# An encoder layer with routed experts on one core: the routing of a batch of tiles in two parts, the second part issued three tiles later

## The chip, the cores and the metric

The kernel runs on one core of a Trainium2 chip. The metric is the device time of one execution in microseconds (us); lower is better. The engines are TensorE (PE, with the weight loads PEld beside it), VectorE (DVE), ScalarE (ACT), GpSimd (POOL) and SyncE (SP, which only issues transfers here). Each runs its own instructions in a fixed order and waits on semaphores for the others. POOL also issues the indirect transfers (gathers and scatters by index).

## The reference, cut to what matters

One layer of an encoder on 2048 tokens of width 1024, float32. What the change touches is the part from the output projection to the choice of experts:

```python
y = jnp.concatenate([mix, mem_out], axis=-1) @ w_out        # 768 -> 1024
x = _layer_norm(DEEPNORM_ALPHA * x + y, ln1_g, ln1_b)
gl = t @ wg + bg                  # 4 groups; the best one is taken
el = (t @ we + be)                # 4 experts per group; the best two of the group
top_v, top_i = lax.top_k(el, 2)
ew = softmax(top_v) * gw          # weight of each of the two
# gate[token, expert] = ew at the two experts, else 0
h = silu(t @ w_gate[e]) * (t @ w_up[e]);  moe += gate[:, e] * (h @ w_down[e])
x = _layer_norm(DEEPNORM_ALPHA * x + moe, ln2_g, ln2_b)
```

There are 16 experts of width 256. `mix` comes from a state-space mixer (S5) and `mem_out` from cross-attention to 256 memory tokens; both lie ahead of the change.

## The kernel before

The tokens are 16 tiles of 128. Matrix products are made of float16 halves: `mm3` (L106) issues three matmuls, high by high (L108), high by low (L109), low by high (L110). The program is recorded by a tile framework that orders the instructions of each engine once, when the program is built, by its own estimate of when each could run; on the chip that order is fixed.

`outproj` (L909) runs a loop of 16 + 2 rounds (L972). Round t issues `project(t)` and, two rounds behind (`LAG` = 2), `score(t - 2)`.

- `project(t)` (L932): 36 matmuls into `poo` (two buffers), then `norm` (L871). For tiles 0 to 12 that is: DVE adds the residual and sums (L881), ACT squares (L886), DVE makes the variance (L887), POOL raises it to -1/2 (`rsa`, L898), DVE makes the bias (L904), ACT scales (L905), DVE multiplies by g (L906), POOL adds b (L907, 128 x 1024). For tiles 13 to 15 DVE does the scaling (L900, L901) and POOL only L898. SP stores the tile to `x1d` in memory.
- `score(t)` (L949): PE transposes the tile (`turn_rows` L982, `ptr`), ACT and DVE copy it to `xT` (for tiles below 12 in two float16 halves, the low one by DVE at L996), PE multiplies by the router's weights (`pl`), DVE adds the bias (`lg`, L961). `pl` has one buffer.

Tiles are routed in batches: (0,4), (4,4), (8,2), (10,2), (12,2), (14,2), as first tile and count. After a batch's last tile `score` calls `route` (L1052). Its first half, some 35 small DVE rows, finds the group and the two experts and ends with the matrix A of ones at the chosen experts (L1112). Then PE multiplies A by a triangle and by ones (L1116 to L1119, into `pp`, one buffer), which gives each pair's place in its expert's list; DVE adds the running counts (`run_cnt`) and works out the places (L1121 to L1144); and POOL scatters the token numbers to the lists in memory, `listd`, two indirect transfers for each tile (L1149): eight for a batch of four, four for a batch of two.

After tile 9 (`EARLY_T` = 10) `early_rows` (L999) loads the lists of two experts (`idx`, SP) and gathers their first 128 tokens each (`xk`, POOL, L1201). `early` (L1006) then transposes them (`ptre`) and runs those experts' first tile ahead of the others; in the fixed order of PE this comes among the scores of the last tiles. `moe` (L1250) loads all lists (`idxall`, `idxrem`) when the last batch has been scattered, gathers the experts' tokens (`xg`, `xr`) and computes the experts (from `ptr` at L1458 on). `pz` (L1260) are two buffers that POOL sets to zero for it.

Of the kernel before, what the change touches and what calls it, by code (L numbers as in the profile page):

```python
# [21 lines left out]
NT = 16  # L22
# [21 lines left out]
EARLY_T = 10  # L44
# [28 lines left out]
class Kern:  # L73
# [32 lines left out]
    def mm3(self, ps, lh, ll, rh, rl, first, last):  # L106
        mm = self.nc.tensor.matmul
        mm(ps, lh, rh, start=first, stop=False)  # L108
        mm(ps, lh, rl, start=False, stop=False)  # L109
        mm(ps, ll, rh, start=False, stop=last)  # L110

    def run(self):
        with ExitStack() as top:
# [795 lines left out]
    def outproj(self):  # L909
        nc, a = self.nc, self.a  # L910
        V = nc.vector
        self.scat, self.oscat, self.sts, self.lds = [], [], [], []
        self.nw = 0
        with ExitStack() as o:
            wp = o.enter_context(self.pool("wout", side="left"))
            kp = self.kp = o.enter_context(self.pool("outk", bufs=2, side="left"))
            ps = o.enter_context(self.pool("psout", bufs=2, space=PSUM))
            self.rps = o.enter_context(self.pool("psr", bufs=1, space=PSUM))
            wh = wp.tile([P, 6, D], F16, name="owh")
            wl = wp.tile([P, 6, D], F16, name="owl")  # L920
            for c in range(6):
                raw = kp.tile([P, D], F32, tag="xres", name=f"oraw{c}")
                nc.sync.dma_start(raw, a["w_out"][:, c])
                (self.split_w_q if c in OWQ else self.split_w)(wh[:, c], wl[:, c], raw)
            g1 = wp.tile([P, D], F32, name="g1")
            b1 = wp.tile([P, D], F32, name="b1")
            nc.sync.dma_start(g1, a["ln1_g"])
            nc.sync.dma_start(b1, a["ln1_b"])
            x1 = {}
            logits = {}  # L930

            def project(t):  # L932
                tk = slice(t * P, t * P + P)
                xr = kp.tile([P, D], F32, tag="xres", name=f"xres{t}")
                nc.sync.dma_start(xr, a["x"][t])
                r = x1[t] = kp.tile([P, D], F32, tag="r1", bufs=4, name=f"r1_{t}")
                po = ps.tile([P, D], F32, tag="po", name=f"poo{t}")
                for c in range(6):
                    if c < 4:
                        lh, ll = self.mh[:, c, tk], self.ml[:, c, tk]  # L940
                    else:
                        lh, ll = self.OTh[:, c - 4, tk], self.OTl[:, c - 4, tk]
                    for n in range(2):
                        ns = slice(n * 512, n * 512 + 512)
                        self.mm3(po[:, ns], lh, ll, wh[:, c, ns], wl[:, c, ns], c == 0, c == 5)
                self.norm(kp, r, xr, WS * ALPHA, po, EPS * WS * WS, g1, b1, f"a{t}", HOW1[t])
                nc.sync.dma_start(self.x1d[tk], r)

            def score(t):  # L949
                whole = t >= WHOLE_T  # L950
                xT = self.turn_rows(x1[t], f"{t}", whole)
                pl = self.rps.tile([P, 20], F32, tag="pl", bufs=1, name=f"pl{t}")
                for c in range(DC):
                    if whole:
                        nc.tensor.matmul(pl, xT[:, c], self.wrf[:, c], start=(c == 0), stop=(c == DC - 1))
                    else:
                        self.mm3(pl, xT[0][:, c], xT[1][:, c], self.wr[0][:, c], self.wr[1][:, c], c == 0, c == DC - 1)
                t0, n = self.batch[t]
                if t == t0:
                    logits[t0] = kp.tile([P, 4, 20], F32, tag="lg", name=f"lg{t}")  # L960
                V.scalar_tensor_tensor(logits[t0][:, t - t0], pl, 1.0 if whole else 1.0 / WS, self.rb, op0=ALU.mult, op1=ALU.add)  # L961
                if t == t0 + n - 1:
                    self.route(kp, logits[t0][:, 0:n], t0, n)
                if t == EARLY_T - 1:
                    self.early_rows(kp)

            self.batch = {}
            for t0, n in BATCHES:
                for t in range(t0, t0 + n):
                    self.batch[t] = (t0, n)  # L970
            LAG = 2
            self.W = [self.expert_weights(self.load_weights(e), e, self.split_w_pool) for e in range(EARLY)]  # L972
            for t in range(NT + LAG):
                if t < NT:
                    project(t)
                if t >= LAG:
                    score(t - LAG)
            for e in range(EARLY):
                self.early(e, ps)

# [71 lines left out]
    def route(self, kp, lg, t0, n):  # L1052
# [4 lines left out]
        def T(shape, dt=F32, bufs=2):  # L1057
            k[0] += 1
            return kp.tile([P] + shape, dt, tag=f"rt{k[0]}", bufs=bufs, name=f"rt{t0}_{k[0]}")

        def first_max(v, shape, m2=None):

            mx = T(shape[:-1])
            V.tensor_reduce(mx, v, axis=AX.X, op=ALU.max)
            eq = T(shape)
            V.tensor_tensor(eq, v, mx.unsqueeze(2).to_broadcast([P] + shape), op=ALU.is_equal)
            V.tensor_tensor(eq, eq, self.w4.unsqueeze(1).to_broadcast([P] + shape), op=ALU.mult)
            m2 = T(shape[:-1]) if m2 is None else m2
            V.tensor_reduce(m2, eq, axis=AX.X, op=ALU.max)
            V.tensor_tensor(eq, eq, m2.unsqueeze(2).to_broadcast([P] + shape), op=ALU.is_equal)  # L1070
            return mx, eq, m2
# [14 lines left out]
        m1, o1, _ = first_max(e1, [n, 4], im[:, :, 0])  # L1086
        e2 = T([n, 4])
        V.scalar_tensor_tensor(e2, o1, -1e30, e1, op0=ALU.mult, op1=ALU.add)
        m2, o2, _ = first_max(e2, [n, 4], im[:, :, 1])
# [20 lines left out]
                            oh.unsqueeze(2).to_broadcast([P, n, 4, 4]), op=ALU.mult)  # L1110
        A = T([n, NE], F16)
        V.tensor_tensor(A, sel[:, :, 0], sel[:, :, 1], op=ALU.add)  # L1112
        pp = self.rps.tile([P, n + 1, NE], F32, tag="pp", bufs=1, name=f"pp{t0}")
        for i in range(n):
            for q in range(i):
# [476 lines left out]
```

## Time and profile before

| | |
|---|---|
| median of 3 executions | 1093.28 us (1093.13 to 1101.6) |
| the profiled execution's own time | 1091.53 us |
| its span, from the first to the last instruction | 1089.7 us |
| PE busy | 899.5 us (83%) |
| PEld busy | 606.8 us (56%) |
| DVE busy | 828.3 us (76%) |
| ACT busy | 540.5 us (50%) |
| POOL busy | 535.3 us (49%) |
| mean granted clock of PE | 0.931 of full speed |
| HBM read, written | 141.95 MB, 58.49 MB |

Times within the trace count from the span's start. In it the projections run from about 488 to 655 us, the last scores and routings to about 702, and the MoE's gathered experts from there to the end. The granted clock is the share of full speed that the chip allowed PE. A wait is shown with its releaser, the row on another engine whose end set the last semaphore; "issue" means that nothing in the profile shows a wait. In a timeline each row has start, length, engine, line, operation, output and inputs, and in square brackets the idle time of the engine just ahead of it. Matmuls overlap, so their pitch is read from their starts.

### The profile page before, as it was taken

The numbers are of one execution on the slowest core, as the hardware profiler recorded it, in microseconds if no ns is written. First come the engines' busy times: TensorE is split into PE (matmuls) and PEld (weight loads), VectorE is DVE, ScalarE is ACT, GpSimd is POOL, SyncE is SP. The second block draws the span as 40 slices with busy tenths as digits, with TensorE's granted clock in tenths as the row PEclk, the third lists the DMA queues.
The fourth block names the chain that finished last, engine by engine and source line by source line (L and its number), as shares of the span: only waits on it lengthen the run. The fifth ranks groups of instructions, "written<-read, shape, count | busy, mean of one in ns | idle before, by whom it ended". The sixth has DMA issues, their size and how long they took to land. (4 is left out here: it accounts for less than half of the span.)

```text
span 1089.7 us, 18757 instructions
## 1 busy us (share of the span) xinstructions
PE 899.5 (83%) x7108; PEld 606.8 (56%) x7108; DVE 828.3 (76%) x1636; ACT 540.5 (50%) x1068; POOL 535.3 (49%) x379
## 2 busy tenths in 40 slices
PE   7777599985845999899999888698979987989880
PEld 4444465674734877444554447476657754755540
DVE  7999888969997666483585676467878787878774
ACT  5122243445748776477633312265656554746530
POOL 1475655426663331325945444525444566367454
PEclk9899799999887999999999987899999998999995
DMA  7113355275271422417736331476578669557531
GB/s 253 41 45 117 121 180 202 69 243 168 61 227 46 132 81 77 140 55 267 257 141 116 78 114 64 142 292 227 206 269 319 215 225 334 198 205 233 208 107 65
DMA packets 65199, 178.14 MB, mean 163 GB/s; under 512 B 15121, under 2 KB 33425, under 8 KB 57681
## 3 DMA queue, kind: packets, MB, share of 16 engines
q1 hardware_dynamic: 44800, 128.83, 36.2%
q0 software_dynamic: 20304, 48.07, 12.9%
q8 instruction: 57, 0.93, 0.3%
q14 instruction: 38, 0.30, 0.1%
HBM read 141.95 MB, written 58.49 MB: 184 GB/s over the span
## 5 line engine op out<-in xcount | busy, mean ns | idle before, releaser
L92 DVE SCALAR_TENSOR_TENSOR wl<-raw,wh 128x1024 f16<-128x1024 f32 x82 | 97.8, 1219 | 10.4 <-ACT wh L91 7.9
L91 ACT ACTIVATE wh<-raw 128x1024 f16<-128x1024 f32 x82 | 82.0, 1048 | 24.1 <-PE pg L109 13.8
L109 PE MATMUL pg<-xl,wh 128*128 128x288 f16 (+1 forms) x256 | 73.3, 288 | 3.0 <-DVE xl L1462 2.8
L110 PE MATMUL pg<-xh,wl 128*128 128x288 f16 (+1 forms) x256 | 73.3, 288 | 0.9 <-issue 0.9
L108 PE MATMUL pu<-xh,wh 128*128 128x288 f16 (+1 forms) x256 | 71.8, 283 | 2.4 <-DVE hl L1049 1.9
L108 PE MATMUL pg<-xh,wh 128*128 128x288 f16 (+1 forms) x256 | 73.5, 289 | 0.0
L1206 POOL DMA_INDIRECT xs<-xg,idxall x31 | 38.9, 1256 | 70.2 <-DVE xg L1499 40.9
L110 PE MATMUL pu<-xh,wl 128*128 128x288 f16 (+1 forms) x256 | 71.6, 282 | 1.5 <-issue 1.5
L109 PE MATMUL pu<-xl,wh 128*128 128x288 f16 (+1 forms) x256 | 71.6, 282 | 0.0
L109 PEld LDWEIGHTS <-wh 128*128 128x128 f16 x576 | 58.1, 101 | 19.0 <-issue 5.7
L108 PEld LDWEIGHTS <-wh 128*128 128x128 f16 x576 | 58.3, 101 | 18.5 <-issue 3.5
L110 PEld LDWEIGHTS <-wl 128*128 128x128 f16 x576 | 57.9, 101 | 17.5 <-issue 4.4
L108 PE MATMUL pq<-xh,S 128*128 128x128 f16 x256 | 51.0, 235 | 15.9 <-DVE OT L295 15.9
L743 POOL TENSOR_TENSOR pe<-pe,ri 128x1024 f32<-128x1024 f32 x16 | 30.3, 1895 | 55.5 <-DVE ri L742 38.8
L108 PE MATMUL pu<-winh,xh 128*128 128x512 f16 x128 | 49.7, 388 | 6.6 <-ACT winh L91 6.6
L1201 POOL DMA_INDIRECT xg<-x1d,idxall x31 | 37.9, 1222 | 32.9 <-DMA out_x<-xg,idxall 13.0
L108 PE MATMUL py<-wh,hh 128*128 128x512 f16 x120 | 45.9, 385 | 8.8 <-ACT hh L1048 4.6
L1462 DVE TENSOR_TENSOR xl<-pt,xh 128x512 f16<-128x512 f32 x60 | 39.5, 683 | 16.1 <-ACT xh L1461 10.1
L1461 ACT ACTIVATE xh<-pt 128x512 f16<-128x512 f32 x60 | 34.0, 592 | 35.8 <-PE pt L1458 29.5
L110 PE MATMUL pq<-xh,S 128*128 128x128 f16 x256 | 51.2, 235 | 0.4 <-DVE S L92 0.3
L1458 PE MATMUL pt<-ident,xg 128*128 128x128 f32 x240 | 37.8, 285 | 16.5 <-DVE xl L1462 7.6
L691 POOL TENSOR_TENSOR m<-S,R 128x1024 f32<-128x1024 f32 x10 | 30.4, 3045 | 42.0 <-DVE S L715 23.6
(471 smaller groups left out, 3163.6 us busy)
## 6 DMA issues: line engine op xcount, KB each, us to landing
raw<-in_w_gate SPq DMA_DIRECT2D x16, 1024.0 KB
raw<-in_w_up SPq DMA_DIRECT2D x16, 1024.0 KB
raw<-in_w_down SPq DMA_DIRECT2D x16, 1024.0 KB
xr<-in_xT SPq DMA_DIRECT2D x16, 512.0 KB
xs<-wo SPq DMA_DIRECT2D x16, 512.0 KB
wol<-xs SPq DMA_DIRECT2D x16, 512.0 KB
M<-kd SPq DMA_DIRECT2D x64, 128.0 KB
xres<-in_x SPq DMA_DIRECT2D x16, 512.0 KB
```

The source lines that it names most:

```text
L91: self.nc.scalar.activation(hi, raw, AF.Copy, scale=WS)
L92: self.nc.vector.scalar_tensor_tensor(lo, raw, WS, hi, op0=ALU.mult, op1=ALU.subtract)
L108: mm(ps, lh, rh, start=first, stop=False)
L109: mm(ps, lh, rl, start=False, stop=False)
L110: mm(ps, ll, rh, start=False, stop=last)
L691: Q.tensor_tensor(m[:, 1], S[:, :, 1::-1], tab(1), op=ALU.mult)
L743: nc.gpsimd.tensor_tensor(pe, pe, ri.unsqueeze(2).to_broadcast([P, 4, 256]), op=ALU.mult)
L1201: return self.nc.gpsimd.indirect_dma_start(out=out, out_offset=None, in_=src, in_offset=bass.IndirectOffsetOnAxis(ap=idx, axis=0))
L1206: st = self.nc.gpsimd.indirect_dma_start(out=self.xs, out_offset=bass.IndirectOffsetOnAxis(ap=si, axis=0), in_=z[:sz], in_offset=None, bou ...
L1458: nc.tensor.transpose(pt[:, i, off:off + sz], x[:sz, (d0 + i) * P:(d0 + i) * P + P], self.ident[:sz, :sz])
L1461: nc.scalar.activation(xh[:, ds_, :n], pt, AF.Copy)
L1462: nc.vector.tensor_tensor(xl[:, ds_, :n], pt, xh[:, ds_, :n], op=ALU.subtract)
```

## The change

`route` becomes a generator that stops after A. `score` runs it to there and puts the rest on a list with the batch's last tile t. Each round of the loop calls `place(t)` between `project` and `score`: the rest of a batch whose last tile lies `LAG` + 3 = 5 rounds back is issued there, so three tiles after the round in which its first part was issued. It is issued inside `issue_after(self.projected)`, which orders the PE instructions of the block behind the last matmul of the projection just issued; `mm3` returns that matmul for it. The early rows are issued with the rest of batch 8. What is left after the loop follows at once (`place(2 * NT)`). The second parts of batches 0, 4, 8 and 10 so come after projections 8, 12, 14 and 15, those of 12 and 14 after all scores. From `route` on, the line numbers of the kernel of after are 14 or 15 higher (L1117 becomes L1132, L1149 becomes L1164, L1201 becomes L1216, L991 becomes L1005).

```diff
@@ mm3
-        mm(ps, ll, rh, start=False, stop=last)
+        return mm(ps, ll, rh, start=False, stop=last)
@@ outproj, project
-                        self.mm3(po[:, ns], lh, ll, wh[:, c, ns], wl[:, c, ns], c == 0, c == 5)
+                        self.projected = self.mm3(po[:, ns], lh, ll, wh[:, c, ns], wl[:, c, ns], c == 0, c == 5).ins
@@ outproj, score
                 if t == t0 + n - 1:
-                    self.route(kp, logits[t0][:, 0:n], t0, n)
-                if t == EARLY_T - 1:
-                    self.early_rows(kp)
+                    rest = self.route(kp, logits[t0][:, 0:n], t0, n)
+                    next(rest)
+                    places.append((t, rest))
+
+
+            def place(now):
+                while places and places[0][0] + LAG + 3 <= now:
+                    t, rest = places.pop(0)
+                    with self.tc.issue_after(self.projected):
+                        for _ in rest:
+                            pass
+                    if t == EARLY_T - 1:
+                        self.early_rows(kp)
+
+            places = []
@@ outproj, the loop
                 if t < NT:
                     project(t)
+                place(t)
                 if t >= LAG:
                     score(t - LAG)
+            place(2 * NT)
@@ route
         V.tensor_tensor(A, sel[:, :, 0], sel[:, :, 1], op=ALU.add)
+        yield
         pp = self.rps.tile([P, n + 1, NE], F32, tag="pp", bufs=1, name=f"pp{t0}")
```

TensorE, around the prefix sums of batch 4 (`pp_6481`), in the kernel before. They stand among the logits of tile 8 (`pl_6605`), and projection 11 (`poo_6635`) goes on behind them:

```order
L109 MATMUL pl_6605<-wr_5311,xT_6590 128x20
L1117 LDWEIGHTS tri
L1117 MATMUL pp_6481<-rt_19_6479,tri 128x16
L1116 LDWEIGHTS ones
L1116 MATMUL pp_6481<-rt_19_6479,ones 128x16
```

In the kernel of after the same sums (`pp_6779`) stand between the last matmul of projection 12 (`poo_6727`) and the transpose of tile 10 (`r_10`):

```order
L109 MATMUL poo_6727<-owl,OT 128x512
L110 LDWEIGHTS OT
L110 MATMUL poo_6727<-owh,OT 128x512
L1132 LDWEIGHTS tri
L1132 MATMUL pp_6779<-rt_19_6479,tri 128x16
```

The sums have moved behind the rest of projection 11 and all of projection 12, and the logits of tile 8 have nothing between them any more.

POOL, in the kernel before, from the power of tile 10 on (of the `listd` rows, x8 are batch 4's lists, the first x4 batch 8's and the second batch 10's; the `rsa` rows shown are the powers of tiles 10, 11, 13 and 14; `xk` are the gathers of the early rows; `pz` the memsets):

```order
L898 TENSOR_TENSOR rsa_6575<-vaa_6577,mhalf 128x1
L907 TENSOR_TENSOR r_10_6537<-r_10_6537,b_5384 128x1024
L1149 DMA listd<-rt_17_6472,rt_28_6520 32768x4 x8
L898 TENSOR_TENSOR rsa_6672<-vaa_6674,mhalf 128x1
...
L898 TENSOR_TENSOR rsa_6961<-vaa_6963,mhalf 128x1
L1149 DMA listd<-rt_17_6769,rt_28_6809 32768x4 x4
L1201 DMA xk_5340<-x1d,idx_6820 128x1024
L1201 DMA xk_5341<-x1d,idx_6820 128x1024
L898 TENSOR_TENSOR rsa_7145<-vaa_7147,mhalf 128x1
L1260 MEMSET pz_7784 128x1024
L1260 MEMSET pz_7786 128x1024
L1149 DMA listd<-rt_17_7055,rt_28_7094 32768x4 x4
```

and in the kernel of after, from the power of tile 12 on:

```order
L898 TENSOR_TENSOR rsa_6764<-vaa_6766,mhalf 128x1
L1164 DMA listd<-rt_17_6472,rt_28_6818 32768x4 x8
L907 TENSOR_TENSOR r_12_6726<-r_12_6726,b_5384 128x1024
L898 TENSOR_TENSOR rsa_6915<-vaa_6917,mhalf 128x1
L898 TENSOR_TENSOR rsa_7058<-vaa_7060,mhalf 128x1
L1164 DMA listd<-rt_17_6715,rt_28_7101 32768x4 x4
L1275 MEMSET pz_7784 128x1024
L1275 MEMSET pz_7786 128x1024
L898 TENSOR_TENSOR rsa_7180<-vaa_7182,mhalf 128x1
L1216 DMA xk_5340<-x1d,idx_7112 128x1024
L1216 DMA xk_5341<-x1d,idx_7112 128x1024
L1164 DMA listd<-rt_17_7009,rt_28_7295 32768x4 x4
```

Batch 4's lists moved from behind tile 10's add to between the power and the add of tile 12 (batch 0's moved likewise, from ahead of tile 7's add to ahead of tile 8's); batch 8's lists moved behind the powers of tiles 13 and 14; the power of tile 15 (`rsa_7180`), which stood behind batch 10's lists, now stands ahead of the gathers `xk`, and batch 10's lists come last of these.

TensorE at the end of the scores, in the kernel before: the logits of tile 15 (`pl_7384`, two halves of four matmuls), the transposes of the gathered rows (`ptre`) and the sums of batch 12 (`pp_7306`):

```order
L955 MATMUL pl_7384<-wr,xT_7371 128x20 x4
L991 MATMUL ptre_0_7486<-ident,xk_5340 128x128 x4
L1117 LDWEIGHTS tri
L1117 MATMUL pp_7306<-rt_19_7304,tri 128x16
...
L955 MATMUL pl_7384<-wr,xT_7371 128x20 x4
L991 MATMUL ptre_1_7493<-ident,xk_5340 128x128 x4
```

and in the kernel of after (`pl_7343`, and `pp_7403` for batch 12):

```order
L955 MATMUL pl_7343<-wr,xT_7330 128x20 x4
L1005 MATMUL ptre_0_7486<-ident,xk_5340 128x128 x4
L955 MATMUL pl_7343<-wr,xT_7330 128x20 x4
L1005 MATMUL ptre_1_7493<-ident,xk_5340 128x128 x4
L1132 LDWEIGHTS tri
L1132 MATMUL pp_7403<-rt_19_7263,tri 128x16
```

The transposes of the gathered rows stay where they stood; the sums of batch 12 moved behind them.

## Rows read from the trace of the kernel before

**Rows 1.** Windows: length, busy PE, PEld, DVE, ACT, POOL; clock; DMA share; GB/s

```profile
655.00:702.00 47.00, 33.76 (x318) 28.69 (x317) 28.40 (x160) 11.63 (x23) 21.23 (x21) 0.79 0.23 69
702.00:1090.00 388.00, 321.05 (x2475) 224.87 (x2473) 299.13 (x464) 205.20 (x361) 197.23 (x160) 0.93 0.64 224
651.00:676.00 25.00, 20.52 (x128) 17.38 (x128) 16.71 (x108) 6.34 (x13) 9.47 (x10) 0.64 0.30 106
```

**Rows 2.** Waits of PE, 488 to 725: total us, times, longest

```profile
PE pp L1117 <- DVE rt L1112: 11.4, 4, 4.8
PE ptr L1458 <- DMA xr<-x1d,idxrem: 7.1, 1, 7.1
```

**Rows 3.** Timeline of PE: start, us, row, idle before; sums and transposes

```profile
600.58 0.17 PE L1117 MATMUL pp<-rt,tri 128*128 128x16 f16 x1 [2.50 <-DVE rt L1112]
...
625.42 0.17 PE L1117 MATMUL pp<-rt,tri 128*128 128x16 f16 x1 [2.56 <-DVE rt L1112]
...
651.60 0.17 PE L1117 MATMUL pp<-rt,tri 128*128 128x16 f16 x1 [4.82 <-DVE rt L1112]
...
668.76 1.09 PE L991 MATMUL ptre<-ident,xk 128*128 128x128 f32 x4
...
701.52 1.94 PE L1458 MATMUL ptr<-ident,xr 128*128 128x128 f32 x8 [7.05 <-DMA xr<-x1d,idxrem]
```

**Rows 4.** Timeline of PE: matmuls of projections 11, 12 and 15

```profile
602.26 0.63 PE L108 MATMUL poo<-owh,OT 128*128 128x512 f16 x1
602.68 0.63 PE L109 MATMUL poo<-owl,OT 128*128 128x512 f16 x1
...
614.25 0.38 PE L109 MATMUL poo<-owl,OT 128*128 128x512 f16 x1
614.47 0.38 PE L110 MATMUL poo<-owh,OT 128*128 128x512 f16 x1
...
654.67 0.63 PE L110 MATMUL poo<-owh,OT 128*128 128x512 f16 x1
```

**Rows 5.** Timeline of POOL: lists, add of tile 12, gathers, memsets, power of tile 15

```profile
606.60 1.03 POOL L1149 DMA_INDIRECT listd<-rt,rt  x1 [2.24 <-DVE rt L1144]
...
615.53 0.96 POOL L1149 DMA_INDIRECT listd<-rt,rt  x1 [0.30 <-issue]
...
628.28 2.35 POOL L907 TENSOR_TENSOR r<-r,b 128x1024 f32<-128x1024 f32 x1 [3.27 <-issue]
...
641.52 0.96 POOL L1149 DMA_INDIRECT listd<-rt,rt  x1 [0.30 <-issue]
647.28 0.98 POOL L1201 DMA_INDIRECT xk<-x1d,idx  x1 [4.79 <-DMA idx<-listd]
...
655.37 1.84 POOL L1260 MEMSET pz<- 128x1024 f32 x2 [5.24 <-PE poo L110]
...
663.15 0.59 POOL L898 TENSOR_TENSOR rsa<-vaa,mhalf 128x1 f32<-128x1 f32 x1
...
684.09 1.04 POOL L1149 DMA_INDIRECT listd<-rt,rt  x1 [6.10 <-DVE ovs_le L1187]
...
695.64 0.98 POOL L1201 DMA_INDIRECT xr<-x1d,idxrem  x1 [0.48 <-issue]
```

**Rows 6.** Timeline of DVE: a held row, logits, scaling of tile 15, last list row

```profile
602.24 2.34 DVE L1128 TENSOR_TENSOR rt<-rt,rt 128x64 f32<-128x64 f32 x2
...
616.56 0.18 DVE L961 SCALAR_TENSOR_TENSOR lg<-pl,rb 128x20 f32<-128x20 f32 x1 [6.95 <-PE ptr L991]
...
663.77 1.28 DVE L901 SCALAR_TENSOR_TENSOR r<-r,rsa,b 128x1024 f32<-128x1024 f32 x1 [1.63 <-POOL rsa L898]
...
671.74 0.18 DVE L961 SCALAR_TENSOR_TENSOR lg<-pl,rb 128x20 f32<-128x20 f32 x1
...
683.57 0.24 DVE L1144 SCALAR_TENSOR_TENSOR rt<-rt,tok 128x4 int32<-128x4 f32 x2
```

**Rows 7.** DMA queues, 647 to 651 us: packets, MB, share of 16 engines

```profile
q0 software_dynamic: 145, 0.55, 46.3%
```

## The prediction, made before the changed kernel ran

> **What bounds the kernel now.** I read four views in turn: busy time by stage, the waits of TensorE in the stretch that the change touches, then the timelines of TensorE, GpSimd (POOL) and VectorE (DVE) there. The stage table shows where something can be won: in the stretch from the last projection to the first expert, 655 to 702 us, PE is busy 33.8 of 47 us and its granted clock is 0.79, while the MoE behind it (702 to 1090) keeps PE at 321 of 388 us [rows 1]. The change alters nothing that the MoE computes, so its value is the time by which the MoE's first transpose comes earlier.
>
> From the projections' start to the first expert (488 to 725 us) PE waits 11.4 us in four pieces for the first matmul of a batch's prefix sum (pp): about 1.5 us for batch 0, then 2.50, 2.56 and 4.82 us for batches 4, 8 and 10 [rows 2, 3]. The releaser is A, the last DVE row of the routing's first part. The only other long wait is the 7.05 us for the gathered rows xr at the MoE's door [rows 2, 3].
>
> **What goes.** The four waits: 11.4 us. Behind three of them PE runs at half rate for a while: matmuls of 512 columns start 0.42 us apart at 602.26, against 0.22 at 614.25, which are the levels of 1.2 and 2.4 GHz [rows 4]. I count eight at 0.21 us too much behind batch 4 (1.7 us), about 1.3 behind batch 8, and, as the last row of projection 15 at 654.67 is 0.63 us long like those at 602.26 and not 0.38, about 1.7 behind batch 10 (half of the stretch from 651.60 on); together 4.7 us. The stretch 651 to 676 shows the same as a clock of 0.64 [rows 1]. So PE gets back at most 16.1 us. One further wait goes: tile 15's power (rsa, 663.15) stood on POOL behind the two memsets (655.37) and batch 10's four lists; in the new order no lists of batch 10 stand ahead of it. At most it waited for all four, 5.1 us by the price below, which brings the upper bound to about 21 [rows 5].
>
> **What comes, batch 0 and 4.** No instruction is added on any engine (the returned matmul and the generator exist only while the program is built), but the sums, the small DVE rows and the lists' transfers all move. One list takes 0.96 us and 0.30 us until the next: batch 4's eight start at 606.60 and 615.53, so 1.27 us each, 10.1 us for eight, 5.1 for four [rows 5]. Batch 0's eight now stand ahead of tile 8's bias add and tile 9's power, which DVE awaits in the middle of batch 4's first part, with tile 8's casts behind. So of the 5.7 us at stake around the first two waits (1.5 + 2.5 + 1.7) between 0 and 5.7 come back; I take 3, the middle. Projection 12, which ended at 614.47 + 0.38 = 614.85 [rows 4], then ends at 611.8.
>
> From there to projection 15's end (654.67 + 0.63 = 655.3) it took 40.45 us [rows 4]. Batches 8 and 10 give back 2.56 + 4.82 + 1.3 + 1.7 = 10.4. But batch 4's lists now stand between tile 12's power and its add. The pp matmuls come at 611.8; in the trace the first list follows pp by 606.60 - 600.58 = 6.0 us, of which one DVE row of 2.34 was held while POOL added [rows 3, 5, 6]. DVE has tile 12's sum and square ahead of it, so I set the first list at 621.5 (617.8 if nothing is ahead). The eight end at 631.6, the add (2.35) at 634; before it ended at 628.28 + 2.35 = 630.6 [rows 5]. SP's load of the early lists moves behind loads that wait for projection 15's end, which is in time for lists that come later still. PE comes to tile 12's transpose at about 631 and waits 3 us (bounds 0 and 6). Projection 15 ends at 611.8 + 40.45 - 10.4 + 3 = 644.9, 10.4 us earlier.
>
> **Batch 8, the early rows and tile 15.** Lists of batch 8 start when its second part is through DVE, which has tile 13's scaling in its middle and that waits for the power behind batch 4's add (634 + 0.6, then 1.28 for the scaling and 8.1 us of small rows, by two thirds of the 12.1 us that both parts of a batch of two took from its last logits at 671.74 to the end of the row at 683.57): 644.0 [rows 5, 6]. They end at 649.1. Next on POOL come the memsets, 1.84 us, and tile 15's power, 0.59: 651.5; tile 15 is scaled at 652.8, where before it was 663.77 + 1.28 = 665.05. Its last logits (lg) would follow as before by 671.74 - 665.05 = 6.7 us, at 659.5 [rows 6].
>
> But PE's order puts the second half of tile 15's logits behind the transpose of the gathered rows xk, before and now. Their gather starts one round trip after the last list, 647.28 - 642.48 = 4.8 us: 653.9. How long it takes to land is not shown by itself. The queue moved 0.55 MB by 651, one gather and a little more, 3.7 us after its start at 647.28; the gather xr took from 695.64 to PE's start at 701.52, 5.9 us, with others beside it [rows 3, 5, 7]. I take 4.2, nearer the first since nothing else is on the queue: 658.1, and 2.4 us for four transposes (1.09), the other half of the logits and the row that makes lg: 660.5 [rows 3]. So the wait for xk takes 1.0 us of tile 15's gain (0.5 to 2.7).
>
> The Trainium skill (DMA: Bandwidth & Descriptors, "Anatomy of one DMA — SWDGE (gpsimd) path") gives about 2.0 us fixed and the bytes over 436e9 per second. For 512 KB that is an estimate of 3.2 us, which the trace's 3.7 for a little more allows; by it tile 15 itself would set its logits (659.5) and the time would come out 1.0 us shorter, 1083.1.
>
> **The tail.** From lg at 671.74 to the last batch's DVE row (683.57 + 0.24) were 12.1 us; some eleven more DVE rows of batch 12's second part now stand in between, about 1 us. 660.5 + 13.1 + 0.3 = 673.9 for the first list of batch 14, against 684.09 [rows 5, 6]. The two gathers and the lists of batches 10 and 12 (5.1 us each) fill POOL from 653.9 to 666.6 at the earliest, so POOL itself leaves 7 us there. From that list to the MoE's first transpose it stays 701.52 - 684.09 = 17.4 us [rows 3, 5]. Gain 10.2. PE stands still at three new places (tile 8's casts, tile 12's add, xk: about 3, 3 and 2 us), and half rate may follow there as in [rows 4]; I take off 1 us, about two thirds of what one such wait cost before. **Sum: 9.2 us**; the profiled execution had 1091.53 us with a span of 1089.7 (1.8 lie around it), so 1082.3, and on the median of 1093.28, which is 1.75 higher, 1084.0.
>
> **Rivals.** *A, the waits come back whole.* Lists issue while PE has other work and the add of tile 12 is early enough: 16.1 us of PE less about 1.6 for xk's bound, a gain of 14.5, 1079. For it: the first list could start at 617.8, and then the add is in time. Against it: one POOL queue holds all lists and the adds.
> *B, the wait moves to the POOL block.* DVE stands 6.95 us ahead of tile 9's lg at 616.56, longer than I can derive from what stands ahead of it [rows 6]; one such wait in either of the two stretches that I walk (some 4 us each beyond what I counted) leaves a gain of 1: 1092.
> *C, slower: the round trip of xk.* Early rows used to be fetched from batch 8's lists at 647.28, 16 us before tile 15 was scaled; now 1 us behind it. If batch 8's lists end after about 659, xk lands after 668, and the end is later than before by every us more: with the lists' end at 663, 4 us, 1097. For it: two DVE-POOL-DVE handovers stand ahead of these lists. Against it: my walk has 10 us to spare.
>
> **How the numbers follow.** My forecast (gain 4 to 12, from the bounds of batch 0, tile 12's add and xk: 1081 to 1089.5) gets 0.50, A 0.27, B 0.15, C 0.08. Beyond 1097 or below 1075 hardly anything is left; leaving out half of C and the ends of A, 1076 to 1096 holds some 8 in 10. About 1% (10.9 us) is what a measurement can tell from no change. Faster by over 1%, below 1082.3: all of A and about a fifth of the forecast, 0.37; slower by over 1%, above 1104, would need batch 8's lists to end at 670, half of C, 0.04; within 1%: 0.59.
>
> **What would show it.** No wait of PE at pp; a wait at tile 12's transpose for POOL's add; DVE's scaling of tile 13 waiting for its power near 635; tile 15 scaled near 652.8; a wait of PE for xk that ends near 658; the last batch's first list near 673.9 and xr's transpose near 691.3. A first MoE transpose above 700 would say B or C; one below 688 would say A. If the MoE itself (388 us before) changes by more than 2 us, the premise that it only shifts is wrong.

## The result, and the profile after

The changed kernel takes 1078.0 us (median of 6 executions, 1077.3 to 1085.1) beside 1093.2 for the kernel before (1090.0 to 1101.6): a ratio of 0.989 with a 95% interval of 0.986 to 0.992, so it is 9 to 16 us faster. A second series gave 1083.7 (9 executions) beside 1094.3, ratio 0.990 (0.986 to 0.994). The forecast was 1084.0 and 1076 to 1096.

| | before | after |
|---|---|---|
| profiled execution / its span | 1091.53 / 1089.7 us | 1077.70 / 1075.9 us |
| PE, DVE busy | 899.5, 828.3 us | 896.7, 825.0 us |
| POOL busy | 535.3 us | 537.4 us |
| mean granted clock | 0.931 | 0.931 |

The engines do the same work; what went is waiting. To see where, I cut each profile at two instants: the first matmul of the first projection, and the MoE's first transpose. In the kernel of after, from the timeline of PE (start, length, row, idle before):

```profile
484.92 0.38 PE L108 MATMUL poo<-owh,mh 128*128 128x512 f16 x1
...
686.89 1.97 PE L1473 MATMUL ptr<-ident,xr 128*128 128x128 f32 x8 [5.96 <-DMA xr<-x1d,idxrem]
```

and in the kernel before the first of the two (the second is in [rows 3], at 701.52):

```profile
488.12 0.38 PE L108 MATMUL poo<-owh,mh 128*128 128x512 f16 x1
```

So the profiled execution's 13.8 us are three pieces: 3.2 us ahead of the first projection, where the two programs are the same row for row on every engine; 11.4 us between the two instants (213.4 to 202.0); and 0.8 us lost in the MoE (388.2 to 389.0). I call the middle piece **the stretch**; the experiments are read from it. Times below with a plus sign count from the first projection's first matmul.

The waits of PE in the same window as [rows 2] (line waited at, releaser: total us, times, longest):

```profile
PE ptr L1473 <- DMA xr<-x1d,idxrem: 6.0, 1, 6.0
PE pl L110 <- DVE xT L1010: 2.5, 4, 0.8
PE ptre L1005 <- DMA xk<-x1d,idx: 2.2, 1, 2.2
...
PE ptr L1005 <- POOL r L907: 1.9, 2, 1.5
```

The 11.4 us at pp are gone. Two of the announced new waits stand there: for xk, and for POOL's add at tile 12's transpose, half as long as I had it. The sums now start right behind a projection, with no idle time ahead of them:

```profile
605.75 0.17 PE L1132 MATMUL pp<-rt,tri 128*128 128x16 f16 x1
...
627.27 1.09 PE L1005 MATMUL ptr<-ident,r 128*128 128x128 f32 x8 [1.48 <-POOL r L907]
...
651.84 1.09 PE L1005 MATMUL ptre<-ident,xk 128*128 128x128 f32 x4 [2.19 <-DMA xk<-x1d,idx]
...
664.15 0.17 PE L1132 MATMUL pp<-rt,tri 128*128 128x16 f16 x1 [0.34 <-issue]
```

POOL's timeline, to be set beside [rows 5]: the first of batch 4's lists, tile 12's add, the last of batch 8's lists, the memsets, tile 15's power, the first gather of early rows and the first list of batch 14:

```profile
614.00 1.98 POOL L1164 DMA_INDIRECT listd<-rt,rt  x1 [1.80 <-DVE rt L1159]
...
624.86 2.36 POOL L907 TENSOR_TENSOR r<-r,b 128x1024 f32<-128x1024 f32 x1
...
640.26 1.74 POOL L1164 DMA_INDIRECT listd<-rt,rt  x1 [0.30 <-DVE vaa L887]
642.00 1.86 POOL L1275 MEMSET pz<- 128x1024 f32 x2
643.81 0.57 POOL L898 TENSOR_TENSOR rsa<-vaa,mhalf 128x1 f32<-128x1 f32 x1
647.40 1.02 POOL L1216 DMA_INDIRECT xk<-x1d,idx  x1 [3.02 <-issue]
...
669.48 0.97 POOL L1164 DMA_INDIRECT listd<-rt,rt  x1 [5.45 <-DVE ovs_po L1204]
```

And DVE, beside [rows 6]: the scaling of tile 15, its logits, and the last row of the last batch's first part (A), which the sums at 664.15 use:

```profile
644.41 1.29 DVE L901 SCALAR_TENSOR_TENSOR r<-r,rsa,b 128x1024 f32<-128x1024 f32 x1 [2.06 <-POOL rsa L898]
...
654.49 0.18 DVE L961 SCALAR_TENSOR_TENSOR lg<-pl,rb 128x20 f32<-128x20 f32 x1
...
661.16 0.19 DVE L1126 TENSOR_TENSOR rt<-rt 128x32 f16<-128x32 f32 x1
```

The steps of the forecast, on the common zero (the forecast's instants less 488.1, the rows of after less 484.9):

| us after the first projection's first matmul | before | forecast | after |
|---|---|---|---|
| projection 12 ends | 126.7 | 123.7 | 121.0 |
| first list of batch 4 | 118.5 | 133.4 | 129.1 |
| tile 12's add ends | 142.5 | 145.9 | 142.3 |
| projection 15 ends | 167.2 | 156.8 | 152.1 |
| tile 15 scaled | 176.9 | 164.7 | 160.8 |
| gather of xk starts | 159.2 | 165.8 | 162.5 |
| transpose of xk starts | 180.6 | 170.0 | 166.9 |
| last logits | 183.6 | 172.4 | 169.6 |
| first list of batch 14 | 196.0 | 185.8 | 184.6 |
| MoE's first transpose | 213.4 | 203.2 | 202.0 |

### The profile page after: what moved, and what is told of

Its sections match the earlier page's. It is cut to its first block, busy times and chain, and to the rows that moved or that the text cites. A ratio compares the mean times of both kernels' runs of the same rounds, so it can differ in the third digit from the quotient of the medians.

```text
span 1075.9 us, 18762 instructions
## 1 busy us (share of the span) xinstructions
PE 896.7 (83%) x7108; PEld 607.8 (56%) x7108; DVE 825.0 (77%) x1636; ACT 540.8 (50%) x1068; POOL 537.4 (50%) x379
## 5 line engine op out<-in xcount | busy, mean ns | idle before, releaser
L91 ACT ACTIVATE wh<-raw 128x1024 f16<-128x1024 f32 x82 | 82.0, 1048 | 23.3 <-PE pg L109 12.2
L1216 POOL DMA_INDIRECT xg<-x1d,idxall x31 | 39.2, 1266 | 32.6 <-DMA out_x<-xg,idxall 14.5
L109 PE MATMUL pq<-xl,S 128*128 128x128 f16 x256 | 50.1, 233 | 0.0
L109 PE MATMUL pu<-winl,xh 128*128 128x512 f16 x128 | 49.4, 386 | 0.3 <-DVE winl L92 0.3
```

The lines of the kernel that those rows point to most:

```text
L91: self.nc.scalar.activation(hi, raw, AF.Copy, scale=WS)
L1216: return self.nc.gpsimd.indirect_dma_start(out=out, out_offset=None, in_=src, in_offset=bass.IndirectOffsetOnAxis(ap=idx, axis=0))
```

## Experiments

Each was profiled, and timed against the kernel before. All milestones are from the timelines, as in the table above. "Total" is the ratio to the kernel before with its 95% interval; the kernel before was timed again in each series, and its median ran from 1087.7 to 1094.3 us there, so totals compare as ratios only.

| | proj. 12 ends | proj. 15 ends | last logits | last lists start | MoE starts (the stretch) | MoE's length | total |
|---|---|---|---|---|---|---|---|
| before | 126.7 | 167.2 | 183.6 | 196.0 | 213.4 | 388.2 | |
| before again | 126.5 | 167.1 | 183.4 | 195.9 | 213.2 | 394.7 | 1.002 (0.999, 1.005) |
| after | 121.0 | 152.1 | 169.6 | 184.6 | 202.0 | 389.0 | 0.989 (0.986, 0.992) |
| after again | 121.0 | 152.0 | 169.4 | 186.0 | 203.0 | 390.3 | 0.990 (0.986, 0.994) |
| 0 and 4 at once | 126.8 | 156.9 | 174.4 | 189.6 | 206.6 | 394.2 | 0.994 (0.991, 0.997) |
| held five tiles | 118.9 | 152.1 | 174.4 | 191.6 | 209.6 | 391.6 | 0.994 (0.992, 0.997) |
| held one tile (the program of before, see below) | 126.4 | 167.4 | 183.5 | 196.1 | 214.9 | 395.6 | 1.002 (1.000, 1.004) |
| early rows later, no hold | 127.0 | 158.5 | 173.9 | 187.8 | 205.8 | 398.0 | 1.000 (0.997, 1.003) |
| batch 8 held two tiles | 121.5 | 151.9 | 168.4 | 184.4 | 202.2 | 395.5 | 0.995 (0.992, 0.998) |
| tile 12's add on DVE | 122.5 | 151.9 | 172.1 | 184.0 | 201.9 | 396.1 | 0.996 (0.994, 0.999) |
| early experts last | 120.7 | 151.8 | 166.3 | 177.7 | 210.6 | 396.5 | 0.997 (0.994, 1.000) |
| the same, batches 8 and 12 sooner | 121.6 | 151.8 | 167.7 | 177.8 | 210.8 | 397.2 | 1.001 (0.998, 1.005) |
| second early expert last | 121.0 | 152.0 | 169.5 | 182.4 | 200.8 | 393.9 | 0.994 (0.991, 0.998) |
| the same, batch 8 held two tiles | 121.0 | 151.2 | 167.9 | 183.1 | 200.5 | 398.4 | 0.992 (0.989, 0.996) |

**How far a profile can be trusted.** The two kernels once more, unchanged.

> The changed kernel once more, for a second profile. Theory: the stretch from the first projection to the MoE's first transpose is fixed by the order (202.0 within 1 us), while what lies ahead (484.9 us) and the MoE behind (389.0 us) move by several us from one execution to the next. Rival: the stretch itself varies by as much as the others.

> The kernel before once more, for a second profile. Theory: the stretch is again 213.4 within 1 us, ahead of it 485 to 488 us, and the MoE between 388 and 396. Rival: the changed kernel's lower time ahead of the stretch (484.9 against 488.1) comes from the change: then it is 488 again here.

Both stretches came again: 213.2 after 213.4, and 203.0 after 202.0 (up to the last logits within 0.3). The first projection began at 485.7 in the kernel before and at 487.8 in the changed one, the other way round than in the first pair. So the 3.2 us ahead of the stretch were no effect of the change, and the rival falls. The MoE of the same kernel before took 388.2 and 394.7. The largest single difference between these two that I can name is DVE's wait for one scattered and gathered tile, pzr. Waits of DVE, 700 to 850 us, in the two profiles of before:

```profile
DVE pzr L881 <- DMA pzr<-xs,idxrem: 6.6, 1, 6.6
```

```profile
DVE pzr L881 <- DMA pzr<-xs,idxrem: 10.3, 1, 10.3
```

In the two of after it was 12.2 and 6.8, with MoEs of 389.0 and 390.3, so this wait alone does not set the MoE's length. A difference of 5 us in the total says little from one execution; the stretch says it to 1 or 2 us (a third profile of the same program, below, has 214.9).

**Is it the waits for the sums, and which of them?** Batches 0 and 4 are routed at once, the others held.

```diff
                     next(rest)
-                    places.append((t, rest))
+                    if t in (3, 7):
+                        for _ in rest:
+                            pass
+                        if t == EARLY_T - 1:
+                            self.early_rows(kp)
+                    else:
+                        places.append((t, rest))
```

> Batches 0 and 4 are routed at once, as in the kernel before; batches 8 to 14 are held as in the changed kernel. Measure: the time from the first projection's first matmul to the MoE's first transpose (before 213.4 us, changed 202.0). Theory: the gain is the four waits of TensorE for the sums plus the half rate behind them, less what waits anew; the waits of batches 0 and 4 (1.5 + 2.5 us) and 1.7 us at half rate come back: 207.7, time some 5.7 us above the changed kernel. Rival: the gain comes from GpSimd and VectorE, where the powers of tiles 14 and 15 no longer stand behind the early rows' gather and batch 10's lists; then batches 0 and 4 are worth at most 1 us here: 202 to 203.

The stretch is 206.6, 4.1 above the mean of after's two (202.5). Projection 12 ends where it did before (126.8), 5.8 us later than in after, and PE waits 4.0 us in two pieces for the sums again:

```profile
PE pp L1138 <- DVE rt L1132: 4.0, 2, 2.5
```

So 5.8 us at projection 12 are the first two waits (1.5 and 2.5) and the half rate behind the second (1.7: eight matmuls run 0.42 us apart again), all of it; and the rest of the gain, 6.7 us of the stretch, comes with the batches from 8 on.

**Is a shorter hold enough?** `LAG + 1` in place of `LAG + 3`.

```diff
-                while places and places[0][0] + LAG + 3 <= now:
+                while places and places[0][0] + LAG + 1 <= now:
```

> Every second part is held one tile instead of three. In TensorE's order the sums of batches 4 and 8 then stand in the logits of a tile as in the kernel before, those of batch 10 inside projection 15. Same measure. Theory: the wait of batch 4 (2.5 us and 1.7 at half rate) stays, that of batch 8 is gone since a tile more lies ahead of it, that of batch 10 is gone or small, and the gathers stand ahead of tile 14's power again: 205 to 209. Rival (any hold is enough): 202 to 203.

The stretch is 214.9 and nothing is won, but this run tests neither expectation. With this edit the tile framework gives every engine the same instructions in the same order, with the same semaphores, as in the kernel before: its own estimate puts the rows that were issued a tile later back where they stood. Batch 10's sums, too, stand in the middle of projection 15 in the kernel before, with eight of its matmuls directly on either side. So the run is a third profile of the kernel before, and a hold of one tile was never executed. It is of use all the same: in it PE waits 10.3 us for the sums, 3.8 of them for batch 10's, and DVE's timeline says what that wait hangs on, with the scaling of tile 14 ahead of the rest of that batch's first part:

```profile
PE pp L1132 <- DVE rt L1126: 10.3, 4, 3.8
```

```profile
648.75 1.28 DVE L901 SCALAR_TENSOR_TENSOR r<-r,rsa,b 128x1024 f32<-128x1024 f32 x1 [6.15 <-POOL rsa L898]
```

The power that this row waits for stands on POOL behind the two gathers, which wait 5.18 us for the list to come back from memory:

```profile
645.87 0.98 POOL L1216 DMA_INDIRECT xk<-x1d,idx  x1 [5.18 <-DMA idx<-listd]
647.15 0.95 POOL L1216 DMA_INDIRECT xk<-x1d,idx  x1 [0.30 <-issue]
648.13 0.58 POOL L898 TENSOR_TENSOR rsa<-vaa,mhalf 128x1 f32<-128x1 f32 x1
```

The first profile of the kernel before has the same chain, with POOL's wait of 4.79 us at 647.28 [rows 5]. POOL's power of tile 14, DVE's scaling and A of batch 10 there:

```profile
649.54 0.59 POOL L898 TENSOR_TENSOR rsa<-vaa,mhalf 128x1 f32<-128x1 f32 x1
```

```profile
650.16 1.28 DVE L901 SCALAR_TENSOR_TENSOR r<-r,rsa,b 128x1024 f32<-128x1024 f32 x1 [5.77 <-POOL rsa L898]
651.37 0.18 DVE L1112 TENSOR_TENSOR rt<-rt 128x32 f16<-128x32 f32 x1
```

**So is it the early rows?** The kernel before with one condition changed; nothing is held.

```diff
-                if t == EARLY_T - 1:
+                if t == 11:
                     self.early_rows(kp)
```

> The kernel before with one thing changed: the early rows (load of idx and gathers xk) are issued after tile 11 instead of tile 9, so that on GpSimd they stand behind the powers of tiles 14 and 15 and batch 10's lists. No second part is held. Same measure (before 213.4 and 213.2). Theory: the longest wait of TensorE for the sums, 4.8 to 5.1 us for batch 10, is GpSimd's wait for idx (4.8 us) handed on by the power of tile 14 and the scaling that stands in the middle of batch 10's first part; it goes with the 1.7 us at half rate, projection 15 ends 5 to 6.5 us earlier (167.2 to about 161), and the MoE's first transpose 4 to 6 us earlier, 207 to 209. Rival (the sums are too early in TensorE's order by themselves): the wait stays above 3 us and the measure above 211.

It is: the stretch falls to 205.8, 7.5 below the mean of before's two (213.3), more than expected, because projection 15 ends 8.7 us earlier: batch 10's wait and its half rate went (4.8 and 1.7 us), and of batch 8's 1.1 us and its half rate (1.3) as well. DVE's scaling of tile 14 no longer waits, and PE's waits for the sums are 5.5 us in three pieces, with none above 2.5:

```profile
640.10 1.28 DVE L901 SCALAR_TENSOR_TENSOR r<-r,rsa,b 128x1024 f32<-128x1024 f32 x1 [0.29 <-POOL rsa L898]
```

```profile
PE pp L1117 <- DVE rt L1112: 5.5, 3, 2.5
```

From projection 12's end to projection 15's it is 31.5 us here, 31.1 in after and 40.5 before. So moving the gathers alone gets all but 0.5 us of what the changed kernel gains in this piece. The hold adds little on top: it also takes away the 1.5 us that batch 8's sums still wait here, and pays 1.5 us at tile 12's add for it. Yet the total did not move (1.000); I come back to that.

**Does the way of xk set the end?** First later, then earlier.

```diff
-                while places and places[0][0] + LAG + 3 <= now:
+                while places and places[0][0] + LAG + 5 <= now:
```

> Every second part is held two tiles longer (five tiles instead of three); batch 8's lists and the early rows then follow the last projection, and batch 10's lists stand ahead of the gathers. Same measure. Theory: the sums need no longer hold, so nothing is won, and the gathered rows xk become what TensorE waits for: the gather starts 5 us later than in the changed kernel (batch 10's lists ahead of it), but the logits of tile 15 no longer stand behind the transposes of xk in TensorE's order, so the wait falls on the early experts and the measure is 201 to 204. Rival (round trip of xk decides the end): 5 us or more above 202.0, so 207 or more.

The stretch is 209.6, the rival's number. Projection 15 ends as in after, but the gathers start at 659.78, at +172.7 against +162.5. They stand behind batch 8's lists, which now come right behind batch 4's eight; batch 10's lists, which I expected ahead of the gathers, stand behind them. The first list of batch 8, the first gather and the first list of batch 10:

```profile
648.30 1.03 POOL L1164 DMA_INDIRECT listd<-rt,rt  x1 [0.22 <-DVE rt L1090]
...
659.78 0.98 POOL L1216 DMA_INDIRECT xk<-x1d,idx  x1 [5.72 <-issue]
...
662.32 1.00 POOL L1164 DMA_INDIRECT listd<-rt,rt  x1 [0.30 <-DVE rt L1080]
```

The MoE's first transpose waits only 1.1 us for its rows, since the early experts that use xk end late. The loss is there before: the last lists start 7.0 us later than in after, and 4.8 of these stand at the last logits, which PE issues ahead of the transposes of xk here and where it waits 4.8 us for a DVE row. Its wait for xk, 2.4 us, comes behind them. So most of the loss is not the way of xk, and this run doesn't price the rest of it.

```diff
-                while places and places[0][0] + LAG + 3 <= now:
+                while places and places[0][0] + LAG + (2 if places[0][0] == 9 else 3) <= now:
```

> As the changed kernel, but batch 8's second part and the early rows are held two tiles instead of three. The gather of xk then starts earlier but stands ahead of tile 15's power on GpSimd. Same measure. Theory: TensorE's wait for xk (2.2 us in the changed kernel) goes, 199 to 200, unless tile 14's or 15's power waits behind the gather for the lists to come back (4.8 to 5.4 us): then 203 to 205. Rival (xk costs nothing, tile 15's own work sets its logits): 202.

PE doesn't wait for xk any more and the last logits come 1.2 us earlier, as my term for xk had it. But the stretch stays (202.2, the rival's number without its cause, for tile 15 alone didn't set its logits): the first of the last lists stands at +184.4, as in after. What won 1.2 us was taken back between the logits and the lists. There PE and DVE work on the early experts, and the last sums stand behind their matmuls: in after A is done at 661.35 and the sums start at 664.15.

**What if the early experts stand behind the last sums?**

```diff
@@ route
-            nc.tensor.matmul(pp[:, n], self.ones, A[:, i], start=(i == 0), stop=(i == n - 1))
+            self.summed = nc.tensor.matmul(pp[:, n], self.ones, A[:, i], start=(i == 0), stop=(i == n - 1)).ins
@@ outproj
-            for e in range(EARLY):
-                self.early(e, ps)
+            with self.tc.issue_after(self.summed):
+                for e in range(EARLY):
+                    self.early(e, ps)
```

> As the changed kernel, but TensorE's work on the early experts (transposes of xk and what follows) is ordered behind the last batch's sums. Measure: first projection's first matmul to the MoE's first transpose (changed 202.0 us). Theory: the changed kernel's end hangs on that work twice, by 2.2 us of waiting for xk ahead of tile 15's second half of logits and by about 3 us in which the last sums stand behind early experts' matmuls; both go, the last batch's first list comes 5 to 6 us earlier (184.6 to about 179), and the MoE's first transpose with it, 197, unless the early experts, which start some 20 us later on TensorE, are then still running there: 197 to 202. Rival (VectorE's rows set the end): the list no more than 2 us earlier, 200 to 202.

The step that I expected came (the first of the last lists at +177.7, 6.9 us earlier) and the end went the other way, 210.6. The rows xr now land while PE is still at the early experts. In windows of the two kernels (length, busy PE, PEld, DVE, ACT, POOL, clock, DMA share, GB/s), first after, then this one:

```profile
651.00:681.00 30.00, 24.81 (x250) 20.10 (x250) 17.51 (x113) 3.84 (x11) 12.25 (x14) 0.81 0.11 26
```

```profile
658.00:697.00 39.00, 24.89 (x238) 17.33 (x239) 15.05 (x78) 3.59 (x9) 19.75 (x21) 0.76 0.48 165
```

The same 25 us of PE work, stretched over 39 us. Part of the idle time is a wait for its own DVE rows (one of 4.3 us), and for part of it the profile shows no releaser. The MoE's first gathers run beside it here (DMA share 0.48 against 0.11); whether they slow it is not shown. Ahead of the sums PE now stands idle for 6.8 us:

```profile
659.56 0.20 PE L1133 MATMUL pp<-rt,tri 128*128 128x16 f16 x1 [6.84 <-DVE rt L1117]
```

The early experts are the work that fills the last routing. Delaying the sums by 2.8 us is the price that the changed kernel pays for it.

The same with batches 8 and 12 held two tiles:

```diff
+                while places and places[0][0] + LAG + (2 if places[0][0] in (9, 13) else 3) <= now:
```

> As the kernel with the early experts behind the last sums, and batches 8 and 12 are held two tiles instead of three, so that xk has landed long before and batch 12's small rows stand ahead of tile 15's. Same measure. Theory: as xk no longer stands ahead of anything that the last lists wait for, its earlier start only helps the early experts; batch 12's earlier rows take up to 1 us off VectorE: 0 to 3 us below the kernel it builds on.

210.8: no gain, as the early experts don't wait for xk in either. Then only the second early expert behind the last sums:

```diff
-            for e in range(EARLY):
-                self.early(e, ps)
+            self.early(0, ps)
+            with self.tc.issue_after(self.summed):
+                self.early(1, ps)
```

> As the changed kernel, but TensorE's work on the second of the two early experts is ordered behind the last batch's sums; the first one stays. Measure: first projection's first matmul to the MoE's first transpose (changed 202.0 and 203.0 us in two profiles; with both experts behind, 210.6). Theory: the early experts fill TensorE's wait for the last lists, and what is moved behind that wait comes out at its end; the changed kernel has 6 to 7 us of idle time there, so moving half of the work gives the last lists 2 to 3 us sooner and ends 199 to 205, no clear gain. Rival (the last sums' delay is what counts): 199 or less.

200.8, the last lists 2.2 us sooner and PE's wait for xr up to 8.6 us: as the theory said, no clear gain (after's two have 202.0 and 203.0), with room left on PE. Together with batch 8 held two tiles:

> As the kernel with the second early expert behind the last sums, and batch 8's second part and the early rows held two tiles instead of three. Measure: first projection's first matmul to the MoE's first transpose (changed 202.0 and 203.0, with the second expert behind 200.8). Theory: TensorE's wait for xk (2.3 us) goes as it did with batch 8 sooner, where tile 15's logits came 1.0 to 1.2 us earlier, and the last sums are no longer held by the early experts: 199 to 200. Rival (tile 14's and 15's powers behind the gathers take it back): 201 to 203.

200.5, between the two: the logits came 1.6 us sooner and the last lists didn't.

**The price of the new wait behind batch 4's lists.**

```diff
-HOW1 = ["SSVQ"] * 13 + ["SV"] * 3
+HOW1 = ["SSVQ"] * 12 + ["SSVV"] + ["SV"] * 3
```

> The changed kernel with tile 12's bias add on VectorE instead of GpSimd, where it stood behind batch 4's eight lists. Same measure (changed 202.0 and 203.0). Theory: TensorE's wait of 1.5 us at tile 12's transpose goes, and 1.2 us of VectorE work is added in its place; projection 15 ends 0 to 1.5 us earlier (152.1 to 150.6) and the MoE's first transpose 0 to 1 us earlier. Rival (the lists' block of 10 us is what still holds tile 12 to 15): 3 us or more.

Projection 15 ends at 151.9 (152.1) and the stretch is 201.9. PE's wait is gone, and from projection 12's end to projection 15's it takes 29.4 us (31.1 in after). But projection 12 ends 1.5 us later, because seven of its matmuls ran at half rate. Windows from +110 to +113, with the columns as above, in after and then here:

```profile
594.90:597.90 3.00, 3.00 (x20) 1.87 (x18) 2.37 (x6) 1.62 (x3) 0.74 (x1) 1.00 0.34 137
```

```profile
597.30:600.30 3.00, 3.00 (x9) 1.16 (x8) 1.34 (x3) 0.64 (x1) 0.97 (x1) 0.50 0.32 127
```

PE waits just ahead of them are the same in both (0.8 and 0.7 us), and why the clock fell here is open. So what the lists' block of 10 us costs at tile 12's add is about 1.7 us, not the rival's 3; in this profile the half rate had taken it back by projection 15's end.

**Why some totals don't follow the stretch.** In six kernels the total is 4.0 to 7.4 us worse than the stretch says, and they are those in which the framework put the MoE's last experts in another order: early rows later (stretch 7.5 us shorter, total 0.3), batch 8 held two tiles (11.1 and 5.7), tile 12's add on DVE (11.4 and 4.0), second early expert last (12.5 and 6.2) with its variant (12.8 and 8.3), and early experts last with batches 8 and 12 sooner (2.5 shorter, total 1.5 longer). In POOL's order these differ from the kernel before by 18 or 20 lines there, four of them by the same 20. In after, in "0 and 4 at once" and in "early experts last" it is 14 lines, another order, and in "held five tiles" none; in these four, and in "held one tile", the total follows the stretch within 2.4 us. A total is uncertain by 2 to 4 us.

The profiles show that the loss lies in the part with the other order. In all of them POOL's order is the same from the MoE's start to the last scatter of expert 10's rows to `out_x`. This row in after, and in "second early expert last":

```profile
965.50 0.99 POOL L1257 DMA_INDIRECT out_x<-xg,idxall  x1 [0.30 <-DVE wl L92]
```

```profile
964.72 0.97 POOL L1258 DMA_INDIRECT out_x<-xg,idxall  x1 [0.30 <-DVE wl L92]
```

From the MoE's start to it the six kernels take 276.7 to 282.6 us and the other eight profiles 277.2 to 283.4 (means 279.8 and 280.0). From it to the end of the span the six take 115.8 to 117.6 us and the other eight 110.4 to 114.0 (means 116.7 and 112.6). So some 4 us are lost behind it. The order of the MoE alone was not tried, so which of the moved rows costs them is open, and so is what the shortest stretch, 200.5, would be worth with after's MoE order. None of the kernels tried is faster than the changed one beyond the uncertainty.

## Why the prediction was right, and where its terms were off

- **Direction, size and place** held: the waits of PE at pp went, the time came out of the stretch, and 1078 lies in the range. The forecast's own gain in the stretch, 10.2 less 1, was too small by 2.2 us; the rest of the distance from 1084 to 1078 is the time outside it, which moves by some us from one execution to the next; that the time came so close to A's 1079 is luck. I gave 0.59 to a change within 1% and 0.37 to a faster one, and 1.1% was measured.
- **The first two waits.** I took 3 of 5.7 us, the middle between two bounds. All came back (5.7; the experiment gives 5.8). The reason to expect less was that batch 0's lists hold POOL ahead of tile 8; they did, and what PE waits for was ready all the same.
- **Tile 12's add.** 3 us forecast, 1.48 measured. The lists of batch 4 started 4.3 us sooner than I had them, 2.7 of it because projection 12 ended sooner. The announced wait of DVE for tile 13's power near 635 didn't come: the row stands at 627.80 (631.0 on the clock of before) with no wait ahead of it.
- **Batches 8 and 10.** The sizes (10.4) held: the piece from projection 12 to 15 lost 9.4 with 1.5 of new wait in it. The cause was incomplete. I took the 4.82 us of batch 10 as the sums standing too early in PE's order. It was POOL's wait for the list, 4.79 us in [rows 5], handed on by tile 14's power and a DVE row: the row stood in my own group, and I read it only for the round trip of xk. One changed line of the kernel before gets 8.9 us there.
- **Upper bound and rival A.** A would have 14.5 us, from 16.1 of PE's. At projection 15's end 15.1 were there. On the way to the MoE 3.7 were lost again: 1.1 at xk and 2.6 between the last logits and the last lists. So the end lay between my sum and A. (The MoE's first transpose at 686.89 looks like my sign for A, below 688, but on the clock of before it is 690.1.) The further wait in the upper bound, up to 5.1 us at tile 15's power, was worth 1.0: from projection 15's end to the scaling of tile 15 it took 9.7 us before and 8.7 after.
- **xk.** The gather started one round trip of 5.4 us after the lists (4.8 forecast) and PE went on 4.44 us after its start (4.2 forecast). In the six other profiles in which PE waits for it, it was 4.21 to 4.56. The Trainium skill's formula (DMA: Bandwidth & Descriptors, "Anatomy of one DMA — SWDGE (gpsimd) path") gave an estimate of 3.2 us; the trace doesn't agree for this gather of 128 rows, and its number decides.
- **The tail.** 13.4 us forecast from the last logits to the last lists, 15.0 measured. The eleven DVE rows were priced; that the last sums stand behind early experts' matmuls was not. Before, A ended at 677.99 and the sums started at 679.42, 1.4 us later; after, at 661.35 and 664.15, 2.8.
- **Rival B** didn't come: DVE still idles 6 us ahead of one row of logits, but not on the path. **Rival C** didn't come: batch 8's lists ended at 642.0, which is 645.2 on the clock of before, and it decides from 659 on. With the gathers 10 us later the stretch was 7 us longer, but most of that was there ahead of any wait for xk, so no run shows C's mechanism by itself.
- **"The MoE only shifts"** held in its length (0.8 us longer, against the 2 us that I had set), but not in its order of rows, which changed at the last experts. I hadn't seen that this could happen; in six of the later kernels it cost some 4 us.

## What to carry to other kernels

Follow a long wait back through every engine before pricing its cure: the wait of PE was a wait of POOL for a transfer, two engines away, and one changed line met it (8.7 of the 15.1 us at projection 15's end). Before moving work out from between two waits, ask what it fills; early experts put behind the last sums brought the lists 7 us sooner and the end 8 us later. And where a framework orders the program, read the order that comes out: one edit here left it as it was, and nine, the change itself among them, altered it in a part that they did not touch. Judge small steps by a stretch cut between two fixed rows rather than by the total.

## What the runs showed of the hardware

- In three profiles of one program (before, before again, held one tile) the stretch repeated within 0.3 us up to the last logits and within 1.7 at its end, while the MoE, with its scatters and gathers, took 388.2, 394.7 and 395.6 us; a single wait for a scattered and gathered tile was 6.6 to 10.9 us.
- Behind each wait of PE for the sums of 2.5 us and more in the kernel before, its matmuls of 512 columns started 0.42 us apart and not 0.22, for 2 to 3 us [rows 4]. In after the waits went and the half rate with them, and the 5.7 us at projection 12 are only complete with it. A long wait is not needed for it, though: with tile 12's add on DVE seven matmuls ran so (granted clock 0.50) behind waits of 0.8 and 0.7 us, behind which after ran at full rate.
- A gather of 128 rows of 4 KB by index took 4.2 to 4.6 us from its start on POOL to the matmul that waited for it (seven profiles).
